# Raw rows of w_out in four tiles of their own, and the mix's inputs loaded in another order

## The chip, the cores and the metric

One Trainium2 chip (trn2), one of its cores. The metric is the device time of one execution in microseconds, the median of the runs. The core's engines are TensorE (PE, matrix products; PEld is its weight load), VectorE (DVE), ScalarE (ACT), GpSimd (POOL) and SyncE (SP), whose queue issues nearly all transfers.

## What is computed

Two models one after the other on x [512 tokens, 1024 channels], in fp32. The first block is differential attention beside a pooling branch, then a mixture of 32 experts. The second has two layers, and the change lies in them. A layer of it, cut to what matters:

```python
p = rms_norm_2(x, norm_g) @ w_in            # gate, and the columns of three branches
mix = concat([gdn, mla, rwkv])              # 384 + 384 + 256 channels
x = x + (mix * silu(gate)) @ w_out          # w_out [1024, 1024]
```

gdn is a gated delta rule, mla attention over a latent, rwkv a recurrence over chunks of 64 tokens in both directions. Ahead of the two layers x is `rms_norm(x, final_g)`, the first model's end.

## The kernel before

**Tiling.** Tokens lie in four tiles of 128 (`NT`), channels in eight blocks of 128 rows of w_out, here called k = 0 to 7. A product in fp32 is made as three in a faster format: both sides are split into a high part and a low rest, w into h and lo, the activations y into mh and ml, and `mm3` sums h x mh, lo x mh and h x ml. So each raw block of w_out (128 x 1024, 512 KB) is loaded, copied by ACT to h (L2309), and POOL subtracts: lo = w - h (L2311). For k = 7 DVE does it, late (L2326).

**Order.** PE's order is the program's own: each stage is a Python generator that yields how long its next products wait for others, and `net.weave` fills that time with another generator. The orders of DVE, ACT, POOL and SP are chosen by the scheduler from the dependences, for the whole program; each engine works strictly in its order. SP's queue issues in order too, and an issue that waits holds those behind it.

**The end of a layer.** `third.prepare` (the triangular solve of the third branch: au, stmp, XT, LT; SC, RB and YK are products beside it) is woven with `mla` (scores, their maximum nm, exponents e with sums rs, transposes of e, products mo; each tile goes to DRAM as mixt). Then `third.states`, eight steps of kp, rhs, pu, AKV, kp, ST in turn, is woven with `Mix`: `mix.load(0, 3)`, `mix.rows(3)` for the first branch's blocks (k = 0 to 2), `load(3, 3)`, `ahead()` (k = 6 and 7) and `rows(3)` for mla's; the last two blocks follow with `load(6, 2)`.

**What Mix loads.** `load(0, 3)` has, in program order, the raw blocks of w_out, x's four tiles (xres), in layer 0 final_g (wf) by which DVE scales x's tiles, the gate (768 KB) and the first branch's output from DRAM (mix, 768 KB). The raw blocks go into a tile of two buffers, `self.w`, block k into buffer k % 2, so a third load waits until h and lo of the block two before are made. In `rows`, PE transposes mix (tr), DVE multiplies it by the gate (y, L2361), ACT makes mh, POOL ml, and PE the products, which DVE adds to x (L2378).

Of the kernel before, what the change touches and what calls it, by code (L numbers as in the profile page):

```python
# [8 lines left out]
F32 = mybir.dt.float32  # L9
# [24 lines left out]
def const_arrays():  # L34
    """Arrays that depend on shapes alone."""
# [32 lines left out]
    # transposed: x -> (-x[16:32], x[0:16]) in each 32  # L68
# [4 lines left out]
    # window / count of the pooling windows that the ends cut  # L73
# [29 lines left out]
def mm3(net, out, a, b, start, stop):  # L103
    """out (+)= a.T @ b for a, b in two float32r parts each."""
    net.matmul(out, a[0], b[0], start=start, stop=False)
    net.matmul(out, a[0], b[1], start=False, stop=False)
    net.matmul(out, a[1], b[0], start=False, stop=stop)


class Net:  # L110
    """What the parts of the kernel share."""

    def __init__(self, ctx, tc, cst, xstack):
# [9 lines left out]
        # x, in a pool that xstack closes  # L123
        p = xstack.enter_context(pool(tc, "xres"))
        self.xres = p.tile([128, NT, D], F32, name="xres")
        # a gate of the first block, then the second's first columns of w_in
        self.w0 = p.tile([128, KC, 128], F32, name="w0")
        # factors of norms
# [5 lines left out]
    def more_consts(self):  # L134
        """Those that the first instructions don't need."""
        self.nc.sync.dma_start(self.c[:, 130:], self.cst[:, 130:])

    def matmul(self, out, a, b, **kw):
        """A matmul, and its time on the tensor engine."""
# [7 lines left out]
    def warm(self, psum, n):  # L147
        """Products that nobody reads: the tensor engine's clock is halved after an idle time."""
# [57 lines left out]
class Front:  # L206
    """The first block up to its second norm."""

    def __init__(self, net, ctx, ring, a):
# [16 lines left out]
        # normed x, then q and k, then x, by halves of the columns; x after the branch in two float32r parts takes the  # L226
        # place of these and of v and the pooling branch
# [13 lines left out]
    def loads(self, first):  # L241
        """The small inputs: those for the first norm, and the others."""
# [32 lines left out]
    def ada_rows(self, w):  # L275
        """512 columns of silu(c) @ w_ada, as four partial sums, on partitions 0, 32, 64, 96."""
# [10 lines left out]
    def ada_channels(self, i, ws):  # L287
        """mod[i]: a shift and a scale by channel p * 8 + k, and the norm's weight times 1 + scale."""
# [15 lines left out]
    def ada_gates(self):  # L304
        """The gates' rows, on every partition."""
# [2231 lines left out]
```

## Time and profile before

| | |
|---|---|
| time, median of 3 runs | 1983.79 us (1980.91 to 1987.42) |
| span of the profiled execution | 1989.2 us, 5.4 above that median |
| PE busy | 1766.2 us, 89% |
| DVE busy | 1064.9 us, 54% |
| ACT busy | 574.7 us, 29% |
| POOL busy | 548.0 us, 28% |
| DMA, mean rate over the span | 168 GB/s |

The profiled execution's own time is its span; what little lies around it isn't in the profile. Busy time is counted on each engine alone, and a wait is put down to the instruction that it ended with. The granted clock of PE is given as a share of its full 2.4 GHz: 0.50 is the lower level, 1.2 GHz, and what lies between is a stretch with both.

### The profile page before, as it was taken

How to read it: one execution, taken by the hardware profiler on the slowest of the kernel's cores; microseconds unless marked ns; L12 is line 12 of the kernel's file. 1: busy time of each engine (PE TensorE's matmuls, PEld its weight loads, DVE VectorE, ACT ScalarE, POOL GpSimd, SP SyncE). 2: the span in 40 equal slices, each digit the busy share in tenths (PEclk: the TensorE clock that was granted, in tenths of full speed). 3: DMA queues.
4: the chain of work that ended last, by engine and by line, in shares of the span. 5: the costliest groups of instructions: out<-in, count | busy, mean ns of one | idle time of the engine just before them, and what ended most of it. 6: DMA issues, size and time to landing. Idle time of an engine off the chain costs nothing.

```text
span 1989.2 us, 34102 instructions
## 1 busy us (share of the span) xinstructions
PE 1766.2 (89%) x14010; PEld 1207.4 (61%) x14010; DVE 1064.9 (54%) x2260; ACT 574.7 (29%) x1134; POOL 548.0 (28%) x559
## 2 busy tenths in 40 slices
PE   5999998999999999696889988879886989898887
PEld 3985684444444444375677746657674878466566
DVE  2445434434343333568874467636678853756337
ACT  4354432121221212353230144411442220352312
POOL 1122111010101001254621244524356212452433
PEclk7999999999999999898998988869898999795789
DMA  9824628999999999332341201233322511210322
GB/s 312 228 86 149 236 70 320 395 397 394 402 406 394 396 404 373 115 83 70 104 107 48 75 17 27 57 122 109 106 73 59 154 52 61 58 23 15 116 87 81
DMA packets 243218, 337.10 MB, mean 169 GB/s; under 512 B 92768, under 2 KB 166160, under 8 KB 226224
## 3 DMA queue, kind: packets, MB, share of 16 engines
q1 hardware_dynamic: 241152, 329.88, 48.0%
q10 hardware_dynamic: 1152, 3.22, 0.4%
q8 instruction: 112, 1.84, 0.4%
q0 software_dynamic: 752, 1.76, 0.3%
q14 instruction: 50, 0.41, 0.1%
HBM read 310.84 MB, written 23.99 MB: 168 GB/s over the span
## 4 chain that ended last, share of the span: by engine, by line
PE 35%; DVE 13%; DMA 3%; issue 3%; POOL 2%; ACT 2%; SPq 0%; DVEq 0%; POOLq 0%; ACTq 0%
PE mm L145 21%; PE kp L145 4%; PE pu L145 4%; PE mm L155 2%; PE x L145 2%; DVE au L1340 2%; DVE stmp L1338 2%; PE tr L145 1%; DVE M L1561 1%; PE mo L145 1%; DMA w<-in_w_out_dram 1%; PE tr L155 1%; DVE y L1285 1%; DVE wl L1210 1%; POOL w L2311 1%
## 5 line engine op out<-in xcount | busy, mean ns | idle before, releaser
L145 PE MATMUL gu<-w,XT 128*64 128x512 f32 x1024 | 225.8, 594 | 0.0
L145 PE MATMUL mm<-hh,wh 128*128 128x512 f32 (+1 forms) x464 | 201.5, 434 | 1.5 <-DVE rw L1315 1.3
L145 PE MATMUL mm<-hh,wl 128*128 128x512 f32 (+1 forms) x464 | 187.2, 404 | 0.0
L145 PE MATMUL mm<-hl,wh 128*128 128x512 f32 (+1 forms) x464 | 187.0, 403 | 0.0
L924 POOL TENSOR_TENSOR yl<-y,yh 128x512 fp32r<-128x512 f32 x30 | 38.1, 1270 | 451.3 <-ACT yh L923 451.3
L145 PEld LDWEIGHTS gu<-w,XT 128*64 128x64 f32 x1024 | 72.1, 137 | 142.7 <-issue 135.1
L934 DVE TENSOR_TENSOR xres<-mm,xres 128x512 f32<-128x512 f32 x128 | 79.2, 681 | 90.6 <-PE mm L145 90.6
L1208 ACT ACTIVATE wh<-w 128x1024 fp32r<-128x1024 f32 (+1 forms) x54 | 57.0, 1056 | 199.3 <-PE mm L145 135.3
L145 PE MATMUL mm<-w,hT 128*64 128x512 f32 x512 | 113.4, 595 | 0.7 <-ACT hT L908 0.7
L145 PEld LDWEIGHTS mm<-hh,wh 128*128 128x128 f32 (+1 forms) x464 | 90.5, 195 | 27.0 <-issue 5.1
L2239 POOL TENSOR_SCALAR e<-e,rs 128x512 f32<-128x512 f32 x48 | 79.0, 1650 | 97.7 <-DVE rs L2238 85.1
L145 PEld LDWEIGHTS mm<-hh,wl 128*128 128x128 f32 (+1 forms) x464 | 90.6, 195 | 21.0
L145 PEld LDWEIGHTS mm<-hl,wh 128*128 128x128 f32 (+1 forms) x464 | 91.1, 196 | 17.5 <-DVE hl L1156 0.2
L1210 POOL TENSOR_TENSOR wl<-w,wh 128x1024 fp32r<-128x1024 f32 (+1 forms) x28 | 67.6, 2416 | 113.2 <-ACT wh L1208 112.8
L145 PE MATMUL mm<-wh,hh 128*128 128x256 f32 x320 | 94.0, 294 | 2.2 <-ACT hh L353 2.2
L145 PE MATMUL mm<-wh,hl 128*128 128x256 f32 x320 | 91.2, 285 | 4.3 <-DVE hl L355 4.0
L145 PE MATMUL mm<-w,mh 128*128 128x512 f32 x256 | 88.3, 427 | 6.6 <-ACT mh L2362 5.0
L145 PE MATMUL mm<-wl,hh 128*128 128x256 f32 x320 | 90.8, 284 | 1.6 <-DVE wl L377 1.6
L145 PEld LDWEIGHTS mm<-w,hT 128*64 128x64 f32 x512 | 35.3, 137 | 66.7 <-issue 62.0
L1338 DVE TENSOR_TENSOR stmp<-au 96x60 f32<-96x60 f32 (+29 forms) x120 | 62.2, 518 | 16.3 <-DMA au<-rmud 10.5
L922 DVE SCALAR_TENSOR_TENSOR y<-mm,ws,g2b 128x512 f32<-128x512 f32 x32 | 24.0, 751 | 78.2 <-PE mm L145 78.2
L868 ACT ACTIVATE X<-mm,ws 128x512 f32<-128x512 f32 x32 | 22.0, 688 | 151.4 <-DVE ws L865 128.2
(580 smaller groups left out, 3896.6 us busy)
## 6 DMA issues: line engine op xcount, KB each, us to landing
w<-in_w_gate_dram SPq DMA_DIRECT2D x64, 1024.0 KB, 13.1
w<-in_w_up_dram SPq DMA_DIRECT2D x64, 1024.0 KB, 13.7
w<-in_w_down_dram SPq DMA_DIRECT2D x64, 1024.0 KB, 10.1
w<-in_w_in_dram SPq DMA_DIRECT2D x52, 512.0 KB, 4.0
w<-in_w_ada_dram SPq DMA_DIRECT2D x24, 1024.0 KB, 8.4
w<-in_w_out_dram SPq DMA_DIRECT2D x16, 512.0 KB, 4.1
w<-in_w_in_dram SPq DMA_DIRECT2D x6, 1024.0 KB, 11.9
w<-in_w_out_dram SPq DMA_DIRECT2D x4, 1024.0 KB, 6.3
```

Source lines behind the costliest of these rows:

```text
L145: return self.nc.tensor.matmul(out, a, b, **kw)
L155: return self.nc.tensor.transpose(out, a, ident)
L868: nc.scalar.activation(X[:, 512 * i:512 * i + 512], ps, AF.Copy, scale=ws[:, 1:2])
L922: nc.vector.scalar_tensor_tensor(y, py, ws[:, 0:1], net.g2b[:, hs], op0=ALU.mult, op1=ALU.mult)
L924: (nc.vector if last else nc.gpsimd).tensor_tensor(yl[:, hs], y, yh[:, hs].bitcast(F32), op=ALU.subtract)
L934: nc.vector.tensor_tensor(net.xres[:, t, hs], po, net.xres[:, t, hs], op=ALU.add)
L1208: nc.scalar.activation(h[:, :, :m], w[:, :, :m], AF.Copy)
L1210: eng.tensor_tensor(lo[:, :, :m], w[:, :, :m], h[:, :, :m].bitcast(F32), op=ALU.subtract)
L1285: nc.vector.scalar_tensor_tensor(y[:, lo:hi], ps[:, lo + d:hi + d], cw[:, j, m:m + 1], y[:, lo:hi], op0=ALU.mult, op1=ALU.add)
L1338: nc.vector.tensor_tensor(tv, au[:n, :, j + 1:, j:j + 1].to_broadcast(sh), au[:n, :, j:j + 1, 0:j].to_broadcast(sh), op=ALU.mult)
L1340: nc.vector.tensor_tensor(au[:n, :, j + 1:, 0:j], au[:n, :, j + 1:, 0:j], tv, op=ALU.add)
L2239: nc.gpsimd.tensor_scalar(e, e, rs, None, op0=ALU.mult)
```

## The change

A new class `Raw` holds a pool of four raw tiles ("wo"), on the side of the third branch's tiles, in the memory that `prepare` gives back. It is made between the two weaves and at once loads blocks 0 to 3. At its end, each `Mix.load(k0)` loads the blocks k0 + 4 to k0 + 6 into it. `Mix` loses its two raw buffers, allocates mix ahead of gate, and loads mix and gate first, then makes the weights, then loads x and final_g. The low part of every second block of a call (k = 1 and k = 4) is made by DVE. Nothing that is computed changes.

```diff
+class Raw(dict):
+    def __init__(self, net, ctx, a, l):
+        self.pool = ctx.enter_context(pool(net.tc, "wo", 4, "right"))
+        for k in range(4):
+            self.load(k)
+    def load(self, k):
+        w = self[k] = self.pool.tile([128, D], F32, name="w")
+        self.net.nc.sync.dma_start(w, dram(self.a["w_out_2"], (self.l * D + 128 * k) * D, [[D, 128], [1, D]]))
 class Mix:
+        self.m = p.tile([128, NT * 384], F32, name="mix")
         self.g = p.tile([128, 3, S], F32, name="gate")
-        self.m = p.tile([128, NT * 384], F32, name="mix")
...
-        self.w = p.tile([128, 2, D], F32, name="w")
...
     def weights(self, k, h, lo, eng):
-        w = self.w[:, k % 2]
-        nc.sync.dma_start(w, dram(self.a["w_out_2"], (self.l * D + 128 * k) * D, [[D, 128], [1, D]]))
+        nc, w = self.net.nc, self.raw.pop(k)
...
     def load(self, k0, n, mix=None):
+        if k0 == 0:
+            mix = self.m.rearrange("p (t c) -> p t c", t=NT)
+            nc.sync.dma_start(mix, self.mixd.rearrange("(t p) c -> p t c", p=128))
+        nc.sync.dma_start(self.g[:, :n], self.gated[128 * k0:128 * (k0 + n), :].rearrange("(j p) s -> p j s", p=128))
+        if k0 < 6:
             for j in range(n):
-                self.weights(k0 + j, *self.wp[j], nc.gpsimd)
+                self.weights(k0 + j, *self.wp[j], nc.vector if j == 1 else nc.gpsimd)
...
-        nc.sync.dma_start(self.g[:, :n], self.gated[128 * k0:128 * (k0 + n), :].rearrange("(j p) s -> p j s", p=128))
...
-        elif k0 == 0:
-            mix = self.m.rearrange("p (t c) -> p t c", t=NT)
-            nc.sync.dma_start(mix, self.mixd.rearrange("(t p) c -> p t c", p=128))
+        for k in range(k0 + 4, min(k0 + 7, KC)):
+            self.raw.load(k)
...
             net.weave(prepare, others, until=prepare)
+            raw = Raw(net, third.ctx, a, l)
             net.weave(states, others, until=states)
```

PE's order stays as it is. The other engines' orders are made anew, and differ at these places, among others. A row is a line of the kernel, an instruction and what it writes and reads.

SP's queue at layer 0's mix start (rows are the third branch's ln_g and ln_b), before:

```order
L2028 DMA rows<-in_rwkv_ln_b_dram 128x256
L2332 DMA xres<-xd 128x1024 x2
L2261 DMA mixt_7547<-mo 384x1x128
L2332 DMA xres<-xd 128x1024 x2
L2308 DMA w<-in_w_out_dram 128x1024 x2
L2337 DMA wf<-in_final_g_dram 128x1024
L2340 DMA gate<-gated_7548 128x3x512
L2346 DMA mix<-mixd_7546 128x4x384
L2308 DMA w<-in_w_out_dram 128x1024 x3
```

and now:

```order
L2261 DMA mixt_7547<-mo 384x1x128
L2292 DMA w<-in_w_out_dram 128x1024 x4
L2348 DMA xres<-xd 128x1024 x2
L2261 DMA mixt_7547<-mo 384x1x128
L2348 DMA xres<-xd 128x1024 x2
L2341 DMA mix<-mixd_7546 128x4x384
L2342 DMA gate<-gated_7548 128x3x512
L2353 DMA wf<-in_final_g_dram 128x1024
L2292 DMA w<-in_w_out_dram 128x1024 x4
```

Four raw blocks stand ahead of x now, and behind x's last tiles mix, gate and final_g in this order. In layer 1 it is the same without final_g.

POOL at layer 1's mix start (w is a lo, cl the decays by which ST is scaled), before:

```order
L2311 TENSOR_TENSOR w_17071<-w,w_17067 128x1024
L2311 TENSOR_TENSOR w_17072<-w,w_17068 128x1024
L2056 TENSOR_TENSOR ST<-ST,cl 128x128 x2
L2311 TENSOR_TENSOR w_17073<-w,w_17069 128x1024
L2363 TENSOR_TENSOR ml<-y,mh 128x384 x2
```

and now:

```order
L2322 TENSOR_TENSOR w_17092<-w,w_17089 128x1024
L2056 TENSOR_TENSOR ST<-ST,cl 128x128 x2
L2322 TENSOR_TENSOR w_17094<-w,w_17091 128x1024
L2056 TENSOR_TENSOR ST<-ST,cl 128x128 x2
L2377 TENSOR_TENSOR ml<-y,mh 128x384
L2322 TENSOR_TENSOR w_17096<-w,w_17095 128x1024
L2377 TENSOR_TENSOR ml<-y,mh 128x384
```

The subtraction ahead of the first ml is gone: k = 2 stands a step of ST earlier, and k = 6 (w_17096) behind the first ml. In layer 0 k = 6 stands ahead of the first ml, where k = 2 stood.

DVE where the second group's weights are made, the same in both layers, as a piece of the difference:

```order
-L2378 TENSOR_TENSOR xres<-mm,xres 128x512
+L2392 TENSOR_TENSOR xres<-mm,xres 128x512
+L2322 TENSOR_TENSOR w_11888<-w,w_11885 128x1024
 L2051 TENSOR_SCALAR AKV<-pu 128x256
+L2375 SCALAR_TENSOR_TENSOR y<-mix,gate 128x384
 L2091 TENSOR_TENSOR YK<-pu,YK 128x256
 L2092 TENSOR_TENSOR y<-kp,YK 128x2x2x64
 L2096 TENSOR_REDUCE mean<-y 128x4
-L2361 SCALAR_TENSOR_TENSOR y<-mix,gate 128x384
```

The subtraction for k = 4 stands between an add into x and AKV. That for k = 1 stands likewise, between the second ST and the third rhs.

DVE ahead of one SC in layer 1's solve, before:

```order
L1340 TENSOR_TENSOR au<-au,stmp 128x24x7
L1338 TENSOR_TENSOR stmp<-au 128x184
L1340 TENSOR_TENSOR au<-au,stmp 128x23x8
L2238 RECIPROCAL rs<-rs 128x1
L1338 TENSOR_TENSOR stmp<-au 128x198
L1340 TENSOR_TENSOR au<-au,stmp 128x22x9
L1338 TENSOR_TENSOR stmp<-au 128x210
L1340 TENSOR_TENSOR au<-au,stmp 128x21x10
L1945 TENSOR_TENSOR SC<-x_16350,mk 128x256 x2
```

and now:

```order
L2238 RECIPROCAL rs<-rs 128x1
L1340 TENSOR_TENSOR au<-au,stmp 128x25x6
L1338 TENSOR_TENSOR stmp<-au 128x168
L1340 TENSOR_TENSOR au<-au,stmp 128x24x7
L1338 TENSOR_TENSOR stmp<-au 128x184
L1945 TENSOR_TENSOR SC<-x_16361,mk 128x256 x2
L1947 TENSOR_TENSOR RB<-x_16361,cst 128x128 x2
L1340 TENSOR_TENSOR au<-au,stmp 128x23x8
L1338 TENSOR_TENSOR stmp<-au 128x198
```

Five instructions of the solve that stood ahead of SC stand behind it now.

## Rows read from the trace of the kernel before

**Rows 1.** Waits of PE, layer 0: instruction <- releaser: us in total, times, longest.

```profile
PE tr L155 <- DMA mix<-mixd: 5.9, 1, 5.9
...
PE pu L145 <- DVE AKV L2051: 0.5, 1, 0.5
```

**Rows 2.** Timeline of PE, layer 1's mix start: start us, us, what [idle before].

```profile
1892.82 0.90 PE L155 MATMUL tr<-cst,mix 128*128 128x128 f32 x3 [4.21 <-DMA mix<-mixd]
...
1895.53 1.22 PE L145 MATMUL mm<-w,mh 128*128 128x512 f32 x2 [0.32 <-ACT mh L2362]
1898.51 0.80 PE L145 MATMUL mm<-w,ml 128*128 128x512 f32 x1 [1.76 <-POOL ml L2363]
```

**Rows 3.** Timeline of SP's queue, layer 0's mix start (issues; us is issuing).

```profile
1298.71 1.10 SPq L2332 DMA_DIRECT2D xres<-xd  x2
...
1301.39 0.65 SPq L2340 DMA_DIRECT2D gate<-gated  x1
```

**Rows 4.** DMA issues of 1297 to 1316: count, KB, median us to landing.

```profile
xres<-xd SPq DMA_DIRECT2D x2, 512.0 KB, 5.1
gate<-gated SPq DMA_DIRECT2D x1, 768.0 KB, 10.1
mix<-mixd SPq DMA_DIRECT2D x1, 768.0 KB, 11.5
```

**Rows 5.** Timeline of all engines, layer 0's mix start.

```profile
1307.94 5.62 POOL L2311 TENSOR_TENSOR w<-w,w 128x1024 fp32r<-128x1024 f32 x2 [5.16 <-DMA w<-in_w_out_dram]
...
1309.39 7.64 DVE L2339 SCALAR_TENSOR_TENSOR xres<-xres,r,wf 128x1024 f32<-128x1024 f32 x4 [4.05 <-DMA wf<-in_final_g_dram]
...
1313.65 0.90 PE L155 MATMUL tr<-cst,mix 128*128 128x128 f32 x3 [5.89 <-DMA mix<-mixd]
...
1317.42 0.73 PE L145 MATMUL kp<-ST,KR 64*64 64x64 f32 x16 [2.87 <-DVE ST L2068]
...
1318.16 2.37 POOL L2311 TENSOR_TENSOR w<-w,w 128x1024 fp32r<-128x1024 f32 x1
...
1321.54 0.80 PE L145 MATMUL mm<-w,ml 128*128 128x512 f32 x1 [1.70 <-POOL ml L2363]
```

**Rows 6.** Line 2339, the scalings: count, ns min/median/max, first and last start.

```profile
L2339 DVE SCALAR_TENSOR_TENSOR xres<-xres,r,wf x4: 1272/1622/3356, 1309.4 to 1315.8; 128x1024 f32<-128x1024 f32 x4
```

**Rows 7.** Timeline of DVE, layer 0, where row block 4's weights are made.

```profile
1356.72 0.69 DVE L2378 TENSOR_TENSOR xres<-mm,xres 128x512 f32<-128x512 f32 x1 [1.12 <-PE mm L145]
1357.61 0.42 DVE L2051 TENSOR_SCALAR AKV<-pu 128x256 f32<-128x256 f32 x1 [0.20 <-PE pu L145]
...
1366.09 2.53 DVE L2098 TENSOR_TENSOR y<-y,mean 128x256 f32<-128x256 f32 x1
```

**Rows 8.** Line 2326, DVE's own weight subtraction (one in each layer).

```profile
L2326 DVE TENSOR_TENSOR w<-w,w x2: 1773/1773/1773, 1387.5 to 1964.4; 128x1024 fp32r<-128x1024 f32 x2
```

**Rows 9.** Timeline of POOL, the same place as rows 7.

```profile
1355.84 4.67 POOL L2311 TENSOR_TENSOR w<-w,w 128x1024 fp32r<-128x1024 f32 x2 [5.11 <-ACT w L2309]
...
1365.98 2.35 POOL L2311 TENSOR_TENSOR w<-w,w 128x1024 fp32r<-128x1024 f32 x1
```

**Rows 10.** Waits of PE, layer 1 from 1790 to the end.

```profile
PE mm L145 <- DVE SC L1945: 6.9, 1, 6.9
...
PE mm L155 <- POOL e L2239: 1.6, 1, 1.6
```

**Rows 11.** Timeline of DVE, layer 1, ahead of SC.

```profile
1796.61 0.35 DVE L1340 TENSOR_TENSOR au<-au,stmp 128x184 f32<-128x184 f32 x1
...
1798.87 0.75 DVE L1945 TENSOR_TENSOR SC<-x,mk 128x256 f32<-128x256 f32 x2
```

**Rows 12.** Stretches: us, busy us of PE PEld DVE ACT POOL, granted clock, DMA.

```profile
1246.00:1258.00 12.00, 12.00 (x153) 9.31 (x151) 10.58 (x30) 5.64 (x13) 4.69 (x3) 0.97 0.01 2
1322.00:1332.00 10.00, 10.00 (x61) 7.44 (x60) 1.54 (x3) 0.00 (x0) 1.21 (x3) 0.50 0.11 40
1812.00:1830.00 18.00, 18.00 (x134) 13.40 (x131) 9.14 (x26) 4.82 (x11) 4.69 (x3) 0.50 0.00 1
```

More of the change, by code (lines that the diff above doesn't have):

```diff
@@ L2277, in mla, with __init__ @@
                 yield 0
+class Raw(dict):
+    def __init__(self, net, ctx, a, l):
+        super().__init__()
+        self.net, self.a, self.l = net, a, l
+        self.pool = ctx.enter_context(pool(net.tc, "wo", 4, "right"))
[4 more added lines that the diff above has]
+        self.net.nc.sync.dma_start(w, dram(self.a["w_out_2"], (self.l * D + 128 * k) * D, [[D, 128], [1, D]]))
 class Mix:
-    def __init__(self, net, a, l, mixd, mixt, gated, xd, xstack):
+    def __init__(self, net, a, l, mixd, mixt, gated, xd, xstack, raw):
         tc, nc = net.tc, net.nc
-        self.net, self.a, self.l, self.mixd, self.mixt, self.gated = net, a, l, mixd, mixt, gated
+        self.net, self.a, self.l, self.mixd, self.mixt, self.gated, self.raw = net, a, l, mixd, mixt, gated, raw
         net.xres = xstack.enter_context(pool(tc, "xres")).tile([128, NT, D], F32, name="xres")
@@ L2297, in __init__ @@
         self.wf = p.tile([128, D], F32, name="wf", tag="w6")
-        split = [p.tile([128, D], F32R, name=f"w{j}") for j in range(3)]
-        self.w = p.tile([128, 2, D], F32, name="w")
-        split += [p.tile([128, D], F32R, name=f"w{j}") for j in (3, 4, 5, 7, 8)]
+        split = [p.tile([128, D], F32R, name=f"w{j}") for j in (0, 1, 2, 3, 4, 5, 7, 8)]
         self.wp = [(split[j], split[j + 3]) for j in range(3)]
@@ L2304, in weights @@
     def weights(self, k, h, lo, eng):
-        net, nc = self.net, self.net.nc
-        w = self.w[:, k % 2]
-        nc.sync.dma_start(w, dram(self.a["w_out_2"], (self.l * D + 128 * k) * D, [[D, 128], [1, D]]))
+        nc, w = self.net.nc, self.raw.pop(k)
         nc.scalar.activation(h, w, AF.Copy)
@@ L2316, in ahead @@
         self.weights(6, *self.wq[0], self.net.nc.gpsimd)
+        self.w7 = self.raw[7]
         self.weights(7, w6, None, None)
@@ L2325, in load @@
             h, lo = self.wp[1]
-            nc.vector.tensor_tensor(lo, self.w[:, 1], h.bitcast(F32), op=ALU.subtract)
-        else:
+            nc.vector.tensor_tensor(lo, self.w7, h.bitcast(F32), op=ALU.subtract)
+        if k0 == 0:
[3 more added lines that the diff above has]
+        if k0 < 6:
             for j in range(n):
-                self.weights(k0 + j, *self.wp[j], nc.gpsimd)
+                self.weights(k0 + j, *self.wp[j], nc.vector if j == 1 else nc.gpsimd)
         if k0 == 0:
@@ L2459, in others @@
                 yield from mla(net, a, l, mchd, mixt, tabd)
-                mix = Mix(net, a, l, mixd, mixt, gated, xd, xstack)
+                mix = Mix(net, a, l, mixd, mixt, gated, xd, xstack, raw)
                 for k in (0, 3):
```

## The prediction, made before the changed kernel had run

> **What bounds the kernel now.** I read the page first: TensorE (PE) is busy 89% of the span, so time can be won only where PE stands still or runs at its lower clock. Then the waits of PE, in the two stretches in which the change works: the start of the mix in layer 0 and in layer 1. There the transposes of the mix wait 5.9 us in layer 0 [rows 1] and 4.2 us in layer 1 [rows 2] for the transfer that brings the mix. Next the SP queue and its landings: the mix is issued last, behind x's tiles, two raw tiles of w_out, final_g (layer 0 only) and the gate [rows 3, 4]. Transfers of one queue come in one after another: gate 1301.39 + 10.1 = 1311.5, mix at 1313.6, where PE starts [rows 5], so 768 KB take 2.1 us and 512 KB about 1.4 us.
>
> Last the timeline of each mix start, to see which wait comes behind the one that goes. In layer 0 there are two [rows 5]: PE's kp block waits 2.87 us for ST on VectorE (DVE), which stands behind four scalings of x (7.64 us, begun only when final_g has landed), and the first product with ml waits 1.70 us behind one subtraction of weights on GpSimd (POOL), 2.37 us. In layer 1 there are no scalings; behind the mix comes the same wait for ml, 1.76 us [rows 2].
>
> **Part 1: raw tiles early, mix and gate ahead of the weights, layer 0.** After the change the queue behind x's last tiles is mix, gate, final_g. x's last tile is in by about 1298.71 + 1.10 + 5.1 = 1304.9 [rows 3, 4]; mix 1304.9 + 2.1 = 1307.0, gate 1309.1, final_g 1309.1 + 1.4 = 1310.5. So the 5.89 us wait goes, but not its worth: the same DVE order stands, so ST and the first y stay behind the four scalings, and final_g lands 1.1 us later than now (DVE began at 1309.39). What helps is that POOL's two subtractions (5.62 us from 1307.94, beside the scalings) have moved ahead of 1304, since their rows are there early. The scalings took 1.272 us at best, 1.622 in the median, 3.356 at worst [rows 6]; undisturbed, 4 x 1.272 = 5.1 us, so they end at 1315.6 and kp starts 0.4 us behind as now: 1316.0 against 1317.42. With the median they end at 1317.0 and nothing is won; with final_g in 1 us later the same. Behind it stand, as now, POOL's ST and one weight subtraction (row block 6 instead of 2), then ml. I take **1.2 us** (0 to 1.4). From 1322 on PE was busy 10.0 of 10 us [rows 12], so what is won is kept.
>
> **Part 2: the same, layer 1.** The queue is x, mix, gate; with layer 0's spacing mix is in some 7 us after x's issue, before PE's last kp block ends at 1892.82 - 4.21 = 1888.6 [rows 2]. One thing is new ahead of it: row block 1's subtraction runs on DVE ahead of the third rhs and pushes that chain, 0.4 to 1.3 us (the part of a 1.27 us instruction that the idle time before rhs doesn't hide); I take 0.7. So tr starts at 1889.3, the first product with mh 2.71 us later as now (1895.53 - 1892.82), with 1.22 us of work, and the one with ml at 1893.2, since POOL's subtraction now stands behind ml instead of ahead of it. Now it starts at 1898.51: **5.3 us** (4.7 to 5.6).
>
> **Part 3: a subtraction on DVE ahead of AKV, both layers.** Row block 4's lower part goes from POOL to DVE, and stands there between the add into x that ends at 1356.72 + 0.69 = 1357.41 and AKV, which started at 1357.61 [rows 7] and for which PE already waits 0.5 us [rows 1]. PE's next instruction needs AKV and all others queue behind it, so this lies on the path. The only weight subtraction that DVE runs now, of this shape, took 1773 ns [rows 8], beside a POOL instruction; 1.272 us is the floor of a two-input 128x1024 instruction [rows 6], and a DVE instruction beside a POOL subtraction (2.35 us from 1365.98 [rows 9]) took 2.53 us where AKV's, with as many elements, took 0.42 [rows 7], so 2.1 us more is the far end. 1357.41 + 1.77 = 1359.2 against 1357.61: I take **-1.7 us per layer** (-1.1 to -3.2), nearest to the row of the same shape. That last instruction's delay goes in turn, but PE's work covers it now; I give nothing for it.
>
> The Trainium skill, SBUF — State Buffer, Who interferes with whom, speaks against this part: it calls the port pair of GpSimd and VectorE "an exclusive lock, not a bandwidth split", which a two-input VectorE instruction finds taken until GpSimd's has ended. By it the subtraction waits for POOL's first of two (1355.84 + 2.34 = 1358.18 [rows 9]), ends at 1359.45, and costs 1.9 us rather than 1.7; the sum below would be 5.1 us rather than 5.5. The row of 2.53 us agrees with it, the row of 1.77 us only in part.
>
> **Part 4: the order of DVE ahead of layer 1's mix.** The DVE order is chosen anew for the whole program. At one place PE waits on it: 6.9 us for SC [rows 10]. Five instructions of the triangular solve, from the one at 1796.61 on, stood ahead of SC at 1798.87 and now stand behind it [rows 11]; the other moves ahead of it swap places only. 2.26 us, less an allowance of mine of 0.3 for rs, which stays ahead and now waits for ScalarE, is **1.9 us** (0.5 to 2.2). After that PE runs without a wait until it waits 1.6 us for POOL's e [rows 10]; the solve's transposes, which delayed that e on DVE, now stand earlier, and delay earlier ones instead: **0.5 us** (-0.8 to 1.6).
>
> **At nothing.** Raw loads for row blocks 0 to 3 go out while PE does scores, and nobody waits for them. POOL's two rows of bv move between the e's, into idle time. The weight tiles h6 and h7 run earlier on ScalarE; if block 6's raw tile landed after 1316, mh would wait behind it in layer 0. The last rows' order of adds and YK changes without a wait of PE that I can name.
>
> **Sum.** 1.2 + 5.3 + 1.9 + 0.5 - 2 x 1.7 = **5.5 us faster**. On the profiled execution that is 1989.2 - 5.5 = 1983.7; it lies 5.4 above the median of the runs, 1983.79, so for the median I say 1983.79 - 5.5 = **1978.3 us**, 0.28%. About 0.3% (6 us) is what a measurement of this kernel can tell from no change.
>
> **Rivals.** *The clock comes with it.* After SC's wait the granted clock is at its lower level and stays there: 0.50 in 1812 to 1830 with PE fully busy. The same PE work in layer 0, after a wait as well, had 0.97 by 1246 to 1258 [rows 12]. Shorter by 1.9 us, layer 1's wait may not lose the clock, or lose it for as short a time as layer 0. Then these 18 us of half-clock work shrink by some 8 (not 9: other engines' chains show up): 1970.3 us. For: the two layers differ though PE's order is the same. Against: the wait is still near 5 us, and it was enough in layer 0 to lose it. Chance 0.27.
>
> *DVE becomes the bound (slower).* Block 1's and block 4's subtractions stand on DVE ahead of rhs and AKV, four in all. If each finds a subtraction of POOL's begun, waits it out and costs PE 2.53 + 1.27 = 3.8 us, that is 15.2 us against gains of 1.2 + 5.3 + 0.7 (lost above, now in it) + 2.4 = 9.6: 5.6 us slower, 1989.4 us. It decides from 2.4 us each. For: PE already waits for AKV. Against: two of the four lie where PE waited for the mix anyway, and AKV's neighbour on POOL has started 1.5 us earlier. Chance 0.1.
>
> *Gains that cancel.* Scalings at the median (0), SC's gain eaten by the next SC, which now stands behind more of the solve (0), 2.2 us for each AKV: 5.3 + 0.5 - 4.4 = 1.4 us, 1982.4 us. This is also what is left if the new order doesn't do what it says in layer 0. Chance 0.18. *All waits go* (final_g early enough that 2.87 and 1.70 go too): against it stands that final_g is queued last; 0.05, 1974 us.
>
> **How the numbers follow.** The forecast has 0.40, its own range is 1975 to 1982, and 0.3% cuts it nearly through the middle. Faster by over 0.3%: 0.18 of it + 0.27 + 0.05 = 0.50; slower by over 0.3%: half of the DVE case and a little from elsewhere, 0.07; within: 0.43. The range takes in the clock case and the far ends of part 3: 1968 to 1986.
>
> **What would show it.** In the changed profile: tr without a wait for the mix in both layers; kp waiting for ST near 1316 in layer 0 still; ml without a wait in layer 1, with one in layer 0; PE's wait for AKV grown from 0.5 to 2.2 us twice; SC's wait near 5 us. Wrong would be: no weight subtraction seen in AKV's wait, a wait for SC as long as now, or granted clock of 1.0 from 1812 on.

## The result: slower, and the profile after

The changed kernel takes **1996.6 us** (median; 1991.3 to 2005.5) against 1983.8 us for the kernel before (1974.4 to 1994.1, measured beside it): 1.0059 times as long, 95% interval 1.0035 to 1.0084, or 7 to 17 us slower. The forecast was 1978.3, 5.5 us faster, with a range that ended at 1986.

The profiled execution of the changed kernel happens to be the fastest of its runs, and that of before one of its slow ones. Their spans, 1989.5 and 1989.2 us, so hide the difference, and the traces have to be compared stage by stage. Nearly every row that the prediction asked for is there. The queue of SP in layer 0 has mix and gate ahead of final_g, as in [rows 3] but in another order:

```profile
1300.08 1.11 SPq L2348 DMA_DIRECT2D xres<-xd  x2
1301.23 0.43 SPq L2341 DMA_DIRECT2D mix<-mixd  x1
1301.77 0.45 SPq L2342 DMA_DIRECT2D gate<-gated  x1
1302.33 0.47 SPq L2353 DMA_DIRECT2D wf<-in_final_g_dram  x1
```

The timeline of PE at both mix starts (start us, us, instruction, in brackets the idle time before it and what ended it), to be held against [rows 2, 5]:

```profile
1309.23 0.90 PE L155 MATMUL tr<-cst,mix 128*128 128x128 f32 x3
1317.29 0.73 PE L145 MATMUL kp<-ST,KR 64*64 64x64 f32 x16 [7.16 <-DVE ST L2068]
...
1321.40 0.80 PE L145 MATMUL mm<-w,ml 128*128 128x512 f32 x1 [1.70 <-POOL ml L2377]
...
1357.36 1.93 PE L145 MATMUL pu<-AKV,RB 64*64 64x64 f32 x16 [2.13 <-DVE AKV L2051]
...
1887.63 0.90 PE L155 MATMUL tr<-cst,mix 128*128 128x128 f32 x3
...
1890.81 0.80 PE L145 MATMUL mm<-w,ml 128*128 128x512 f32 x1
```

The transposes `tr` wait for nothing in either layer. In layer 0 the wait has moved to ST, 2.87 to 7.16 us, and `ml` waits 1.70 as before; in layer 1 `ml` no longer waits. The line of 1357.36 is the price that was expected for it: PE's wait for AKV has grown from 0.5 [rows 1] to 2.13 us, and in layer 1, at 1927.04, to 2.14. DVE and POOL there, against [rows 7, 9]:

```profile
1354.38 0.69 DVE L2392 TENSOR_TENSOR xres<-mm,xres 128x512 f32<-128x512 f32 x1 [1.10 <-PE mm L145]
1354.98 1.99 DVE L2322 TENSOR_TENSOR w<-w,w 128x1024 fp32r<-128x1024 f32 x1
1356.89 0.41 DVE L2051 TENSOR_SCALAR AKV<-pu 128x256 f32<-128x256 f32 x1
...
1353.51 2.38 POOL L2322 TENSOR_TENSOR w<-w,w 128x1024 fp32r<-128x1024 f32 x1 [4.88 <-ACT w L2320]
1355.84 1.99 POOL L2377 TENSOR_TENSOR ml<-y,mh 128x384 fp32r<-128x384 f32 x1
```

Block 4's subtraction stands ahead of AKV and takes 1.99 us. What the prediction did not ask for is in the table by stretches of the changed kernel (stretch, us, then busy us of PE, PEld, DVE, ACT and POOL with their instructions, then the granted clock and DMA):

```profile
1347.36:1355.36 8.00, 7.87 (x89) 5.91 (x86) 4.01 (x9) 2.92 (x5) 2.87 (x2) 1.00 0.01 2
1357.36:1365.36 8.00, 8.00 (x96) 8.00 (x98) 4.55 (x6) 0.00 (x0) 3.38 (x3) 0.50 0.28 92
1365.36:1373.36 8.00, 8.00 (x102) 7.88 (x100) 2.35 (x7) 0.00 (x0) 0.61 (x1) 0.50 0.57 106
1373.36:1381.36 8.00, 8.00 (x70) 6.96 (x70) 1.80 (x5) 0.00 (x0) 0.61 (x1) 0.50 0.00 0
1381.36:1389.36 8.00, 8.00 (x31) 6.39 (x31) 7.14 (x21) 0.53 (x1) 1.63 (x2) 0.79 0.00 0
```

Ahead of the wait the granted clock is 1.00 (2.4 GHz). From the product that waited it is 0.50 (1.2 GHz) for 24 us, with PE busy all of that time: nothing waits, so no list of waits shows this loss. In layer 1 it is 0.53 and 0.50 for 16 us from 1927.04:

```profile
1927.04:1935.04 8.00, 8.00 (x101) 8.00 (x101) 4.57 (x6) 0.00 (x0) 3.40 (x3) 0.53 0.21 66
1935.04:1943.04 8.00, 8.00 (x97) 7.88 (x95) 2.63 (x7) 0.00 (x0) 0.61 (x1) 0.50 0.01 2
```

In the kernel before, the clock was 1.00 for 24 us behind AKV in both layers, of which these are the first 8:

```profile
1358.10:1366.10 8.00, 8.00 (x162) 7.84 (x164) 4.14 (x11) 2.11 (x2) 6.38 (x6) 1.00 0.59 194
...
1935.10:1943.10 8.00, 8.00 (x163) 7.84 (x164) 4.18 (x11) 2.12 (x2) 6.38 (x6) 1.00 0.63 197
```

From this product to the last rows' first product with mh, PE needed 33.0 us in each layer before, and 43.8 and 39.9 us now.

To compare stages over all kernels I use three stretches: **mix 0** and **mix 1**, from the first kp<-ST,KR of a layer to the product that waits for the last rows' mh; and **solve 1**, from the product of layer 1 that waits 1.94 us for M to the start of mix 1, where the triangular solve runs on DVE.

| kernel | median us | mix 0 | mix 1 | solve 1 | clock behind AKV, layers 0, 1 (first 8 us) |
|---|---|---|---|---|---|
| before | 1983.8 | 102.1 | 102.4 | 82.4 | 1.00, 1.00 |
| before_again (the same code) | one run: 1982.1 | 104.5 | 100.6 | 70.2 | 1.00, 1.00 |
| after | 1996.6 | 110.8 | 98.7 | 73.4 | 0.50, 0.53 |
| k4_pool | 1979.6 | 98.7 | 92.4 | 76.1 | 1.00, 1.00 |
| all_pool | 1979.1 | 98.8 | 92.1 | 74.4 | 1.00, 1.00 |
| fill | 1986.0 | 102.7 | 96.9 | 75.0 | 1.00, 1.00 |
| before_k4 | 2007.6 | 109.0 | 113.1 | 77.7 | 0.56, 0.51 |
| half_k4 | 1986.1 | 112.3 | 96.5 | 65.7 | 0.50, 0.58 |
| wf_first | 1970.4 | 98.6 | 95.3 | 70.4 | 1.00, 1.00 |
| raw_only | 1969.9 | 103.7 | 94.5 | 65.9 | 1.00, 1.00 |
| order_only | 1987.4 | 102.6 | 101.4 | 73.3 | 1.00, 1.00 |
| after_cp | 1988.4 | 110.9 | 95.9 | 68.6 | 0.50, 0.56 |
| before_cp | 1987.6 | 104.4 | 97.4 | 71.9 | 1.00, 1.00 |
| all_pool_cp | 1972.0 | 102.0 | 94.3 | 68.4 | 1.00, 1.00 |

Medians are over many runs. They come from four series, in which the kernel before itself took 1983.8 us (beside after), 1983.7 (beside k4_pool, all_pool, fill and before_k4), 1982.7 (beside half_k4, wf_first, raw_only and order_only) and 1981.1 (beside the last three); across series the ratio to before is the better measure. Stretches are from one execution each; the same code differs by 2 to 3 us in a mix stage (before and before_again), and by far more in solve 1, on which see below.

### The profile page after: what moved, and what is told of

Its sections match the earlier page's. It is cut to its first block, busy times and chain, and to the rows that moved or that the text cites. A ratio compares the mean times of both kernels' runs of the same rounds, so it can differ in the third digit from the quotient of the medians.

```text
span 1989.5 us, 34105 instructions
## 1 busy us (share of the span) xinstructions
PE 1769.8 (89%) x14010; PEld 1216.0 (61%) x14010; DVE 1073.3 (54%) x2264; ACT 574.1 (29%) x1134; POOL 544.3 (27%) x555
## 3 DMA queue, kind: packets, MB, share of 16 engines
q0 software_dynamic: 752, 1.76, 0.3%
## 4 chain that ended last, share of the span: by engine, by line
PE 34%; DVE 14%; issue 3%; DMA 2%; ACT 2%; POOL 1%; SPq 0%; DVEq 0%; POOLq 0%; ACTq 0%
PE mm L145 20%; PE kp L145 4%; PE pu L145 4%; DVE au L1340 2%; PE x L145 2%; PE mm L155 2%; DVE stmp L1338 2%; PE tr L145 1%; DVE M L1561 1%; PE mo L145 1%; PE tr L155 1%; DVE wl L1210 1%; DVE y L1285 1%; DMA au<-mud 1%; DVE nm L2234 1%
## 5 line engine op out<-in xcount | busy, mean ns | idle before, releaser
L145 PE MATMUL mm<-wh,hh 128*128 128x256 f32 x320 | 94.3, 295 | 2.2 <-ACT hh L353 2.2
## 6 DMA issues: line engine op xcount, KB each, us to landing
w<-in_w_in_dram SPq DMA_DIRECT2D x6, 1024.0 KB, 12.2
```

The source lines that it names most:

```text
L145: return self.nc.tensor.matmul(out, a, b, **kw)
```

## The experiments

Theory 1: the subtraction ahead of AKV makes PE wait 1.6 us longer, and that costs the clock behind it, some 10 us per layer. Theory 2, the rival: the wait costs only itself, and the loss is somewhere else.

**Undone alone: k4_pool.** The changed kernel with block 4's lower part back on GpSimd.

```diff
-                self.weights(k0 + j, *self.wp[j], nc.vector if j == 1 else nc.gpsimd)
+                self.weights(k0 + j, *self.wp[j], nc.vector if k0 + j == 1 else nc.gpsimd)
```

> The changed kernel with one thing undone: the low part of row block 4 goes back from VectorE to GpSimd; that of block 1 stays on VectorE. Theory 1 (the subtraction ahead of AKV makes PE wait 2.1 us, the granted clock falls to its lower level there, and the products behind it run at half speed for some 25 us): PE's wait for AKV back at 0.5 us, clock 1.0 from AKV to the layer's end, about 10 us of clock and 1.6 us of wait won back in each layer, so about 1996.6 - 23 = 1974 us. Theory 2 (the subtraction costs its wait only, and the loss is made elsewhere, at the mix's start or in layer 1's solve): 3 us won back, about 1993 us.

Measured: 1979.6 us, 0.9988 of before (0.9962 to 1.0015), 17 us below the changed kernel (14 by the two ratios). The timeline of PE and DVE and the stretches behind AKV:

```profile
1355.17 1.14 PE L145 MATMUL pu<-AKV,RB 64*64 64x64 f32 x16 [0.52 <-DVE AKV L2051]
...
1353.80 0.69 DVE L2392 TENSOR_TENSOR xres<-mm,xres 128x512 f32<-128x512 f32 x1 [1.12 <-PE mm L145]
1354.69 0.42 DVE L2051 TENSOR_SCALAR AKV<-pu 128x256 f32<-128x256 f32 x1 [0.20 <-PE pu L145]
```

```profile
1355.20:1363.20 8.00, 7.35 (x145) 7.13 (x145) 4.95 (x10) 0.32 (x1) 6.29 (x5) 1.00 0.12 8
1363.20:1371.20 8.00, 8.00 (x126) 7.14 (x125) 3.79 (x11) 0.00 (x0) 1.23 (x2) 1.00 0.96 206
```

The wait is 0.52 again, the clock stays at 1.00, and the 16 products that took 1.93 us take 1.14. The two mix stages are 12.1 and 6.3 us shorter than in the changed kernel. Theory 1's sign and mechanism hold; the time is 5.6 us above its 1974.

**Done alone: before_k4.** The kernel before, with block 4's lower part on DVE and nothing else.

```diff
-                self.weights(k0 + j, *self.wp[j], nc.gpsimd)
+                self.weights(k0 + j, *self.wp[j], nc.vector if k0 + j == 4 else nc.gpsimd)
```

> The kernel before with one thing done: the low part of row block 4 on VectorE instead of GpSimd, nothing else. Theory 1 (clock): PE waits about 2 us for AKV in both layers, half clock behind it, 1984 + 2 x (1.6 + 10) = 2007 us. Theory 2 (wait only): 1984 + 3 = 1987 us.

Measured: 2007.6 us, 1.0139 of before (1.0102 to 1.0176), 24 us slower. The two mix stages hold 6.9 and 10.7 us of it; the rest lies elsewhere, and the scheduler has also given layer 1's solve another order here (see below). Its wait for AKV and the 25 us behind it in each layer:

```profile
1359.06 1.20 PE L145 MATMUL pu<-AKV,RB 64*64 64x64 f32 x16 [2.13 <-DVE AKV L2051]
```

```profile
1359.10:1384.00 24.90, 24.90 (x279) 23.00 (x280) 11.47 (x24) 3.69 (x4) 7.90 (x8) 0.66 0.55 144
1936.70:1962.00 25.30, 25.29 (x265) 23.82 (x266) 8.78 (x19) 3.17 (x3) 6.99 (x6) 0.50 0.24 81
```

Clock 0.66 and 0.50, as Theory 1 says; Theory 2's 1987 is out.

**The wait kept busy: fill.** The changed kernel with five products that nobody reads, ahead of the product that waits for AKV. DVE is as late as in the changed kernel; only PE does not stand still.

```diff
+                    for _ in range(5):
+                        net.matmul(fill[:, 0], net.ident, net.c[:, :512], start=True, stop=True)
```

> The changed kernel with five products that nobody reads (128x128 by 128x512, about 0.45 us each at full clock) issued on PE ahead of the one that waits for AKV, in each layer. The subtraction and its delay of AKV stay. Theory 1 (clock): PE has work while it waits, the clock stays at 1.0 behind it, some 10 us won per layer less what the fillers add beyond the wait (0.3 us each layer): about 1977 us. Theory 2 (wait only): the fillers add 0.3 us per layer at most and win nothing: about 1997 us.

Measured: 1986.0 us, 1.0021 of before (0.9998 to 1.0045), 10.6 us below the changed kernel. The timeline of PE in layer 0, and the stretches behind AKV in both layers:

```profile
1351.80 4.56 PE L145 MATMUL kp<-cst 128*128 128x512 f32 x10
1356.29 1.14 PE L145 MATMUL pu<-AKV,RB 64*64 64x64 f32 x16
```

```profile
1356.30:1364.30 8.00, 8.00 (x136) 7.31 (x136) 4.61 (x11) 0.00 (x0) 1.08 (x2) 1.00 0.64 159
1364.30:1380.00 15.70, 15.70 (x169) 13.65 (x170) 8.97 (x21) 1.05 (x2) 3.82 (x5) 1.00 0.27 54
1919.00:1944.00 25.00, 24.47 (x305) 21.23 (x305) 15.53 (x42) 1.05 (x2) 5.06 (x7) 1.00 0.13 42
```

The fillers were too long, 4.56 us where the wait is 2.13 (0.91 each, where 0.45 was expected), so each layer loses up to 2.4 us more than without them, and still the kernel is 10.6 us faster, with the clock at 1.00; the mix stages are 8.1 and 1.8 us shorter than in the changed kernel. This is the run that tells the idle time from the late data: the subtraction is where it was, and the loss is gone.

**Half of it: half_k4.** Columns 0:512 of block 4's subtraction on DVE, the others on GpSimd.

```diff
+        if k == 4:
+            for e, cs in ((nc.vector, slice(0, 512)), (nc.gpsimd, slice(512, 1024))):
+                e.tensor_tensor(lo[:, cs], w[:, cs], h[:, cs].bitcast(F32), op=ALU.subtract)
```

> The changed kernel with the k=4 subtraction split: its columns 0:512 stay on DVE ahead of AKV, 512:1024 go to GpSimd; the k=1 subtraction stays on DVE. PE's wait for AKV should come to 1.1 to 1.4 us, between the 0.5 of before and the 2.1 of the changed kernel. Theory 'the wait alone costs': 2 x 0.8 us above k4_pool, 1981 us, and no drop of the clock behind AKV. Theory 'any longer wait there loses the clock': granted clock near 0.5 behind AKV in both layers and 1994 to 1997. Theory 'there is a point between': clock 1.0 behind AKV with a wait of 1.2 but 0.5 with 2.1, so 1980 to 1983, or one layer of each, about 1987.

Measured: 1986.1 us, 1.0001 of before (0.9978 to 1.0025). The half took 1.46 us, so the wait came to 1.60 and 1.61 us and not the 1.1 to 1.4 expected, as the timeline of DVE and PE and the stretch behind AKV in layer 0 show:

```profile
1363.20 1.46 DVE L2323 TENSOR_TENSOR w<-w,w 128x512 fp32r<-128x512 f32 x1
...
1365.04 1.75 PE L145 MATMUL pu<-AKV,RB 64*64 64x64 f32 x14 [1.60 <-DVE AKV L2051]
```

```profile
1365.00:1373.00 8.00, 7.96 (x95) 7.96 (x97) 4.55 (x6) 0.00 (x0) 4.65 (x4) 0.50 0.31 79
```

The clock was lost in both layers, and mix 0 is as long as in the changed kernel (112.3 against 110.8): no saving by halves at this place. Yet the time is 10 us below the changed kernel, which neither theory gives. The table has it outside the mix: solve 1 is 65.7 us against 73.4.

**Both subtractions undone: all_pool.** Blocks 1 and 4 on GpSimd.

```diff
-                self.weights(k0 + j, *self.wp[j], nc.vector if j == 1 else nc.gpsimd)
+                self.weights(k0 + j, *self.wp[j], nc.gpsimd)
```

> The changed kernel with the low parts of row blocks 1 and 4 both on GpSimd, as before. Theory 1: as k4_pool for block 4; block 1's subtraction no longer delays the third rhs on VectorE (0.7 us each layer), but then GpSimd makes one more ahead of the first ml: 1974 us, within 3 us of k4_pool. Theory 2: about 1993 us.

Measured: 1979.1 us, 0.9993 (0.9965 to 1.0021), the same as k4_pool. Block 1's subtraction on DVE costs next to nothing: it takes 1.22 us, nearly all in time in which DVE would have waited, and PE's wait for the third rhs is 0.74 us with it and 0.57 without.

**The loads, taken apart: raw_only and order_only.** The first has the four early raw tiles with the old order of loads and all subtractions on GpSimd. The second is the kernel before, its two raw buffers and all, with mix and gate loaded ahead of the weights. Raw_only against the changed kernel, in `Mix.load`:

```diff
-        if k0 == 0:
-            mix = self.m.rearrange("p (t c) -> p t c", t=NT)
-            nc.sync.dma_start(mix, self.mixd.rearrange("(t p) c -> p t c", p=128))
-        nc.sync.dma_start(self.g[:, :n], self.gated[128 * k0:128 * (k0 + n), :].rearrange("(j p) s -> p j s", p=128))
...
-                self.weights(k0 + j, *self.wp[j], nc.vector if j == 1 else nc.gpsimd)
+                self.weights(k0 + j, *self.wp[j], nc.gpsimd)
...
+        nc.sync.dma_start(self.g[:, :n], self.gated[128 * k0:128 * (k0 + n), :].rearrange("(j p) s -> p j s", p=128))
...
+        elif k0 == 0:
+            mix = self.m.rearrange("p (t c) -> p t c", t=NT)
+            nc.sync.dma_start(mix, self.mixd.rearrange("(t p) c -> p t c", p=128))
```

Order_only against the kernel before, in the same function, at whose end these loads stood:

```diff
+        if k0 == 0:
+            mix = self.m.rearrange("p (t c) -> p t c", t=NT)
+            nc.sync.dma_start(mix, self.mixd.rearrange("(t p) c -> p t c", p=128))
+        nc.sync.dma_start(self.g[:, :n], self.gated[128 * k0:128 * (k0 + n), :].rearrange("(j p) s -> p j s", p=128))
-        else:
+        if k0 < 6:
             for j in range(n):
                 self.weights(k0 + j, *self.wp[j], nc.gpsimd)
```

> The four raw tiles beside the third branch alone: loads of the mix in the old order (x, final_g, gate, mix last), all subtractions on GpSimd. Theory R (the gain of 10 us in layer 1's mix and 1.5 in layer 0's come from the weights being split early, and from two fewer transfers ahead of the mix): tr still waits for the mix, by 2 to 4 us, the wait for ml is gone in layer 1, time about 1980. Theory O (the order of mix and gate carries them): tr waits as before, 5.9 and 4.2 us, and the time is that of before, 1983 to 1984.

> The kernel of before with its two raw buffers, and only the mix's load order changed: mix and gate ahead of the weights and final_g. Theory O: tr's waits of 5.9 and 4.2 us go, time about 1979 to 1980. Theory R: the weights now land behind mix and gate, GpSimd's subtractions come later and ml or the product behind it waits longer by what tr no longer waits, so 1983 to 1985.

Measured: raw_only 1969.9 us, 0.9940 of before (0.9916 to 0.9964); order_only 1987.4, 1.0026 (0.9998 to 1.0055). PE's waits at the start of order_only's mix 0:

```profile
1311.76 0.80 PE L145 MATMUL mm<-w,mh 128*128 128x512 f32 x1 [2.27 <-ACT mh L2362]
1313.78 0.80 PE L145 MATMUL mm<-w,mh 128*128 128x512 f32 x1 [1.22 <-POOL w L2311]
1315.71 0.79 PE L145 MATMUL mm<-w,ml 128*128 128x512 f32 x1 [1.14 <-POOL ml L2363]
...
1324.23 0.80 PE L145 MATMUL mm<-w,mh 128*128 128x512 f32 x1 [3.58 <-POOL w L2311]
```

With the order alone the wait for mix goes and comes back as waits for POOL's subtractions, whose raw rows are now later: mix 0 is 102.6 us against 102.1, mix 1 101.4 against 102.4. (The 1.0026 is no measure of the loads: this kernel has the changed kernel's order of the solve, and before_cp below, with that order and the old loads, has 1.0033.) With the early raw tiles alone mix 1 falls to 94.5, most of what it can gain; mix 0 does not (103.7), since DVE's scalings of x now stand ahead of an AKV for which PE waits 5.6 us. With both together mix 0 is 98.6 to 98.8 in three kernels (k4_pool, all_pool, wf_first), but 102.0 in all_pool_cp, so that layer 0 takes both is likely and not shown.

**final_g earlier: wf_first.** k4_pool with final_g ahead of mix in layer 0.

```diff
+        if k0 == 0 and self.l == 0:
+            nc.sync.dma_start(self.wf, dram(self.a["final_g"], 0, [[0, 128], [1, D]]))
         if k0 == 0:
             mix = self.m.rearrange("p (t c) -> p t c", t=NT)
```

> The changed kernel with both k=4 subtractions back on GpSimd (as k4_pool, 1979.56 us) and, in layer 0, final_g issued ahead of mix instead of behind the gate. It asks whether the wait of 7.2 us for ST in layer 0, which stands behind the four scalings of x that wait for final_g, is worth anything. Theory W (final_g is the bound there): it lands about 2.5 us earlier or more, the scalings end near 1311 to 1313 and the first kp block behind tr starts 3 to 5 us earlier: about 1975. Theory Q (something else stands behind it: the tile h6, whose raw rows land near 1316 and behind which ScalarE's mh is queued, or mix, which now lands 0.7 us later): no change, 1979 to 1980.

Measured: 1970.4 us, 0.9916 of before (0.9881 to 0.9951). By its time Theory W would be confirmed, and it would be wrong: mix 0 took 98.6 us, and 98.7 without the edit. The timeline of DVE and PE shows why:

```profile
1306.08 4.87 DVE L2356 SCALAR_TENSOR_TENSOR xres<-xres,r,wf 128x1024 f32<-128x1024 f32 x4 [3.33 <-DMA wf<-in_final_g_dram]
1310.87 0.42 DVE L2051 TENSOR_SCALAR AKV<-pu 128x256 f32<-128x256 f32 x1
...
1311.34 0.47 PE L145 MATMUL kp<-AKV,BK 64*64 64x64 f32 x2 [6.94 <-DVE AKV L2051]
```

The scalings do begin earlier, but the scheduler has put them ahead of an earlier AKV, and PE waits 6.94 us for that instead of 7.45 for ST. Layer 0 gains nothing; the 9 us are somewhere else again.

**The order of the solve.** half_k4, raw_only and wf_first have one thing in common that none of their edits names. PE's order is written out and the same in all kernels (fill's five products aside), but DVE's is chosen by the scheduler, and in these three the steps of layer 1's triangular solve stand among the other work in the order that layer 0 has. The changed kernel, before, and k4_pool with all_pool have three other orders, fill and before_k4 share a fifth, and order_only has the changed kernel's. So the whole times of kernels with different orders differ by more than their edits, and the readings above rest on the mix stages and the clock in them. Copies of a small tile onto itself on GpSimd ahead of layer 1's third branch turn one order into another and leave the loads and the subtractions as they are (4 copies in after_cp, 8 in before_cp, 3 in all_pool_cp). They are not quite neutral: GpSimd makes them in layer 0's mix, where PE's waits for ST and ml grow by 1.3 us in before_cp (to 3.14 and 2.74) and by 0.6 in after_cp, and some of DVE's instructions change places outside the solve too, most of them near 1500 to 1600 us. The edit of after_cp:

```diff
             third = Rwkv(net, a, l, rw, lk)
+            for _ in range(4 * l):
+                nc.gpsimd.tensor_copy(net.r1, net.r1)
```

> The changed kernel with four copies of a 128x4 tile onto itself on GpSimd ahead of layer 1's third branch; nobody needs them. Their only effect on the order: the triangular solve of layer 1 stands on DVE in the order that it has in layer 0 (and in the kernels raw_only, wf_first and half_k4), no longer in the changed kernel's own. Both subtractions stay ahead of AKV, so the clock falls there as before. Theory 'the order of the solve is worth 8 to 10 us' (half_k4 1986.08 against 1996.6 though both lose the clock behind AKV, wf_first 1970.42 against k4_pool 1979.56): 1986 to 1989. Theory 'the order is worth nothing, those kernels differ in something else': 1996 to 1997.

> The kernel of before with eight such copies on GpSimd ahead of layer 1's third branch; they put layer 1's solve on DVE into exactly the order that it has in the changed kernel, and the loads and subtractions of the mix stay as they were. Theory 'the order of the solve': the changed kernel is 12.8 us slower than before, of which its two mix stages hold 5.0 in the profiles (layer 0 110.8 against 102.1, layer 1 98.7 against 102.4), so the order holds up to 8: 1988 to 1992. Theory 'the order is worth nothing': 1983 to 1984.

> all_pool (the changed kernel's loads, both subtractions back on GpSimd, 1979.09) with three such copies on GpSimd, which give layer 1's solve the order of layer 0. If both causes add up, no wait behind the subtraction and the better order: 1968 to 1971, as raw_only and wf_first. If the order is worth nothing: 1979.

Measured: after_cp 1988.4 us (1.0029 of before, 1.0004 to 1.0053) where the changed kernel has 1996.6; before_cp 1987.6 (1.0033, 1.0010 to 1.0057) where before, in the same series, has 1981.1; all_pool_cp 1972.0 (0.9942, 0.9914 to 0.9970) where all_pool has 1979.1. In all three the time moves in the direction expected, by 6 to 8 us by medians and 6 to 10 by the ratios, while the clock behind AKV stays lost in after_cp. In before_cp DVE has the changed kernel's order of the solve, without any of its edits. Only before_cp stands in one series with the kernel that it is compared with, and its interval leaves out 1; the intervals of after_cp and of the changed kernel overlap.

That a new order in layer 1 moves the whole time is shown by before_cp; that the solve is the place is argued. For it: solve 1 takes 65.7 to 70.4 us in the five kernels with layer 0's order, and 71.9 to 82.4 in the others but for before_again (70.2). Against it: in before_cp's profile solve 1 takes 71.9 us, between the 82.4 and the 70.2 of before's two, and it is the stretch from mix 0's end to solve 1 that is longer, 397.8 us against 392.2 and 392.3.

**Before once more: before_again.**

> The kernel of before, unchanged, profiled once more: how much of its layer 1 is the execution's own. In the first profile the stretch from the product that waits for M to the first output product of layer 1 took 82.4 us with the clock at 0.50 from 1799 to 1839. If the order alone sets it, the stretch takes 81 to 84 again; if the execution does (the clock comes back sooner in some), it differs by 5 us or more, with the clock.

Measured: 1982.1 us, and solve 1 took 70.2 us against 82.4. In both executions PE waits 6.9 us for SC, [rows 10] and again, and the clock falls. The stretches behind that wait, first of before, then of before_again:

```profile
1799.20:1815.20 16.00, 15.86 (x124) 12.07 (x124) 12.27 (x35) 4.29 (x10) 4.70 (x3) 0.50 0.04 13
1815.20:1839.20 24.00, 24.00 (x141) 17.11 (x140) 11.28 (x36) 6.91 (x16) 4.75 (x3) 0.50 0.02 9
```

```profile
1804.40:1812.40 8.00, 7.83 (x70) 6.21 (x70) 7.48 (x23) 2.91 (x7) 1.56 (x1) 0.50 0.08 25
1812.40:1820.40 8.00, 8.00 (x90) 5.37 (x88) 6.17 (x18) 2.73 (x6) 3.13 (x2) 0.84 0.01 2
1820.40:1836.40 16.00, 15.89 (x149) 10.98 (x142) 12.43 (x39) 8.68 (x20) 7.87 (x5) 1.00 0.22 60
```

The same program after the same wait had 0.50 for 40 us in one execution, and in the other was at 0.84 after 8 us and at 1.00 after 16. So the 82.4 us of the first profile were largely the execution's own, and solve 1 of a single profile is no measure of an order: for that the many runs above count.

**The account.** Against before, by stages: the loads save 3.4 us in mix 0 and 10.0 in mix 1 (k4_pool; 5.8 and 8.2 against before_again), together 13 to 14. That is an estimate from single executions: in before_cp, which has none of the loads' edits, mix 1 is 5.0 us shorter than in before. The subtraction ahead of AKV costs, in the table, 12.1 + 6.3 = 18.4 us (17.0 by medians; k4_pool undoes it, with another order of the solve), of which 1.6 us per layer is wait and some 15 the clock (43.8 - 33.7 and 39.9 - 34.9 behind AKV). That makes 18.4 - 13.4 = 5.0 us slower; against before_cp, which has the same order of the solve, the changed kernel is 0.26% or 5 us slower by the ratios, though their intervals overlap. The new order costs 6.5 us, measured side by side (before_cp; 2 to 11), of which 1.3 us are the copies' own. In sum 5.0 + 6.5 - 1.3 = +10.2 us, where 12.8 (7 to 17) was measured; what is missing isn't placed.

## Why the prediction was wrong, step by step

**The step that failed** is in part 3: the subtraction "lies on the path", and its price was set equal to the length of the wait, -1.7 us per layer. The length was right: the wait grew by 1.61 and 1.62 us (2.13 and 2.14 less 0.52), with DVE's instruction at 1.99 us beside the 1.77 taken from [rows 8]. (The prediction's own figures give 1359.18 - 1357.61 = 1.57, of which it made 1.7.) What PE lost behind it was not in the sum: 10.1 us of clock in layer 0, 5.0 in layer 1. With these, 5.5 us faster becomes 9.6 us slower, and that is within the measured interval. That the rest of the sum then fits is luck: part 2 brought more than forecast, and part 4 a loss in place of a gain. The material was at hand. [rows 12] show PE fully busy at 0.50 for 18 us behind a wait, and the first rival was built on just that, but only where the change *shortened* a wait. The step to make was the same question at the place where the change *lengthened* one: what runs behind it, and what would that cost at half the clock? The 24 us behind AKV ran at 1.00 before; 24 us at half the clock do what 12 us do at the full one, so up to 12 us per layer were at stake.

The Trainium skill (SBUF — State Buffer, Who interferes with whom) was weighed in the same part, and the 1.9 us worked out from it, against 1.7, was the smaller question. (The words that the prediction quotes stand on the same page, in the section SBUF: two separate sides.) The rows agree with it nearly: the subtraction began at 1354.98, in the middle of POOL's (1353.51 + 2.38 = 1355.89), and ended 1.08 us after it, where undisturbed ones of the same line took 1.22; POOL's `ml` then took 1.99 us, and 0.99 in k4_pool.

**Part 1** (1.2 us) came out at its size. From the first kp to `tr` it is 18.8 us in place of 24.6, and from `tr` to the product with ml 12.2 in place of 7.9: 1.5 us, by the mechanism described, ST behind four scalings, which took 4.87 us. The size alone proves little, since the same stretch took 32.5 us in before and 35.0 in before_again; the mechanism is in the rows. Without the AKV loss the rest of mix 0 gave another 2 us.

**Part 2** (5.3 us) had the right mechanism and too small a size: 27.2 to 19.5 us up to `tr` and 5.7 to 3.2 from there to ml, 10.2 us; against before_again 8.3, and 6.2 against before_cp, whose order of the solve is the changed kernel's. The mis-sized term is the one ahead of `tr`. It was taken as the 4.2 us of wait less 0.7; the products before it also ran faster than in the first profile, whose clock was 0.58 in the 8 us from 1863.2, when the changed kernel had 1.00 from 1866.8. So much of the excess is the clock with which the stage began, and not the loads. Block 1's subtraction, put at 0.7, cost 0.17 (all_pool).

**Part 4** (1.9 + 0.5 us faster) had the wrong sign. The wait of 6.86 us for SC is gone in the changed kernel, where PE reached that product late and at the lower clock (0.50 from 1794.3 to 1811.4); in its place the next SC is waited for, 3.73 us. The same order alone, in before_cp, shows the term as it was meant and what became of it. First the changed kernel, then before_cp:

```profile
1822.35 3.30 PE L145 MATMUL mm<-vt,SC 64*64 64x64 f32 x32 [3.73 <-DVE SC L1945]
```

```profile
1807.57 3.31 PE L145 MATMUL mm<-vt,SC 64*64 64x64 f32 x32 [5.10 <-DVE SC L1945]
...
1821.03 1.90 PE L145 MATMUL mm<-vt,SC 64*64 64x64 f32 x32 [0.80 <-DVE SC L1945]
...
1829.34 1.90 PE L145 MATMUL mm<-vt,SC 64*64 64x64 f32 x32 [1.14 <-DVE SC L1945]
```

The wait falls by 1.76 us, close to the 1.9 of the forecast, and the next two SC, for which PE did not wait before, take 1.94 back. In the changed kernel POOL's e is also waited for twice, 1.28 and 2.57 us where it was 1.58 once, and rhs for 1.13; with the changed kernel's order alone the time is 6.5 us longer, 1.3 of it by the copies. The step that failed is to price a new order of a whole stretch by the one wait that stands out in it.

**The rivals.** The clock decided, as in the first rival, at another place and with the other sign. That rival's own sign was there too, a granted clock of 1.00 from 1811.4 to 1821.6, but before_again shows it without the change (1.00 from 1815.0 to 1842.3), so it can't be laid to the change. "Gains that cancel" was right that the next SC would eat SC's gain, which before_cp shows, and wrong on what AKV costs. "DVE becomes the bound" named the right instruction and the right side, but not the mechanism: it put 3.8 us on each of four subtractions, and two cost nothing, the others some 9. The list of what would show the forecast right was met nearly line by line (`tr`, ST near 1316, ml, AKV 2.2 us twice) by a kernel that is slower: it named waits alone, and a clock is not a wait.

**What stays open.** Why the order is worth some 5 to 10 us is not settled: PE's waits of over 1 us in solve 1 sum to 9.0 us in the changed kernel and to 10.8 in after_cp, which is the quicker, and the clock there differs from execution to execution. Whether it is the solve's order that counts, or another stretch of layer 1, is open as well. What a wait between 0.52 and 1.60 us ahead of the first output products costs was not tried.

## What to carry to other kernels

An instruction placed ahead of something that PE waits for can cost far more than the wait it makes (some 15 us of clock for 3.2 of wait here): read the granted clock of the stretch behind it, and price that stretch at 0.50. Where such a wait can't be removed, products that nobody reads can hold the clock, and pay even when they are longer than the wait. And a change of time under a scheduler is not yet evidence for the edit: wf_first gained 9 us at a place that its edit didn't touch, and only the stage's own length told.

All kernels with early raw tiles, no subtraction ahead of AKV and layer 0's order of the solve are faster than both kernels: raw_only 1969.9, wf_first 1970.4, all_pool_cp 1972.0 us, 0.6 to 0.8% below before.

## What the hardware showed that was not expected

A wait of 1.60 to 2.15 us ahead of the 64x64 output products took the clock from 1.00 to 0.50 in all eight places where it stood (two each in after, after_cp, half_k4 and before_k4), for 17 to 27 us. A wait of 0.52 at the same place left it at 1.00 for the next 8 us in all eighteen. A second wait, of 0.65 to 0.79 us and some 7 us behind the first, stood in ten places; it left the clock at 1.00 in nine, and in raw_only's layer 1 (0.77 us) it was 0.50 for 3.4 us.

Length alone does not decide. Ahead of the last rows' products with mh, of 512 columns, PE waited 2.08 to 2.36 us in seventeen places: the clock stayed at 1.00 behind ten of them, as in both layers of before, and was 0.50 for 3.4 us behind seven. Of eleven waits of 1.41 to 1.47 us there, two were followed by 0.50 for 3.4 us. Here is one of 2.35 us in before, then what followed 1.6 us behind one of 2.31 in k4_pool:

```profile
1391.06 0.73 PE L145 MATMUL mm<-w,mh 128*128 128x512 f32 x2 [2.35 <-ACT mh L2362]
...
1391.00:1396.00 5.00, 4.87 (x21) 3.70 (x22) 1.93 (x5) 1.31 (x5) 1.42 (x2) 1.00 0.29 105
```

```profile
1390.40:1393.80 3.40, 3.40 (x11) 2.54 (x10) 0.94 (x3) 0.72 (x2) 0.00 (x0) 0.50 0.29 106
```

The second surprise is how long the lower level lasts: 40 and some 10 us after the same wait of the same program. The spread of a kernel's runs goes with the mean clock (before: 32 runs in one series, from 1972 us at 0.918 to 2002 us at 0.901); how much of it comes from such stretches is not shown.
